# A retention and attention trunk: the ring tiles of split weights start at a place that moves by 16 bytes from product to product

## The chip, the cores and the metric

One core of a Trainium2 chip runs the whole kernel. The time is the device time of one execution in microseconds, from start to end; it is stated as the median of several runs. One more execution was taken with the hardware profiler, and all rows of traces come from that one.

## The reference

Two requests of 512 tokens and width 1024 pass through two layers with the same weights, each `x = x + Mixer(RMSNorm(x))`, and a last RMSNorm. All is fp32.

```python
def diff_attention(h, w_in, lq1, lk1, lq2, lk2, subln_g, w_out, lambda_init):
    proj = h @ w_in                                    # 1024 -> 8192
    q, k, v, gate = jnp.split(proj, [...], axis=-1)
    q = rotary_half(q...) * (DA_HEAD_DIM ** -0.5);  k = rotary_half(k...)
    ...
        p = jax.nn.softmax(s, axis=-1).reshape(B, N_HEADS, 2, Q_BLOCK, S)
        a = (p[:, :, 0] - lam * p[:, :, 1])
        return jnp.einsum('bhqk,bkhe->bqhe', a, v)
    ...
    o = rms_norm(o, subln_g, SUBLN_EPS) * (1.0 - lambda_init)
    return (o * jax.nn.silu(gate)) @ w_out              # 2048 -> 1024

def bidir_retention(h, w_in, decay_fwd, decay_bwd, subln_g, w_out):
    proj = h @ w_in                                    # 1024 -> 6144
    ...
    o_f = retention_direction(q, k, v, log_g_f, True)
    o_b = jnp.flip(retention_direction(flipped q, k, v, log_g_b, False), 1)
    o = rms_norm(o_f + o_b, subln_g, SUBLN_EPS)
    return (o * jax.nn.silu(gate)) @ w_out
```

## The kernel before

**Split operands.** A product of two fp32 matrices is made of three passes in the type float32r. Each operand is split into a high part (a copy on ScalarE, `hi_of`, L400) and a low part (source less high part on VectorE, `lo_of`, L403), and `PASSES` at L32 names the pairs: high by high, high by low, low by high. A matmul on TensorE has a stationary operand, 128 x 128, that a weight load brings in, and a moving one, 128 rows of 256 or 512 columns.

**The two projections.** A unit (`Unit`, from L518 on) is a block of 256 columns of a layer's input weights for both requests. It is computed by seven products P1 to P7 in place of eight, in the manner of Strassen and Winograd: sums of blocks of the activations (B11, B21, T1 to T4, made by `make_b` and kept split in 28 slots for the whole stage) by sums of blocks of weights. `prep` loads the raw weights by DMA, forms the sum in a tile `st` on VectorE (L558) and splits it into tiles of the ring `ws`, of `WS_BUFS` = 7 places with 1024 floats to a partition. `product` issues the matmuls. A "pair" unit has both parts in one ring tile, as the stationary operand, and the activations move, 512 columns (L599, twelve matmuls to a product). A "wide" unit has a ring tile for each part, the activations are stationary, and the ring tiles move, 256 columns (L609, 48 to a product). `evac` takes the sums out of PSUM, through ScalarE copies `c` and VectorE sums `e` (L644), a ring of eight tiles; gates, rotated q and k, and v go out to DRAM.

**Attention and retention.** The first layer goes through head, request and 128 tokens: scores (L1116), softmax, transposes (L1161), weighted sums (L1181). The second goes through blocks of head and request, in two halves of 256 tokens: `state2` (L1339), `score2` (L1315), `av2` (L1359, L1367). Both end in `out_step` (L891), with oT stationary and the split output weights moving, 512 columns: `out_weights` splits these into two ring tiles of `ws` per head and half.

**Where tiles lie.** Pools are laid one behind the other: `sm`, `cp`, `ar`, `wk`. `ar` holds one large tile, the arena, of 18 slots of 1024 floats; `slot` gives a view into it, which starts at

```python
        lo = 32 + at * 1024 + shift
```

with a `shift` in floats: 16 (64 bytes) for the first layer's k and v, 16 and 32 for the second's q and k, 32 for oT (`new_oT`, L826). A slot with a shift reaches into the next one, which `b.also` tells the planner. Other slots, such as those from 20 on, and constants are tiles of `cp`; the rings are tiles of `wk`, made by `view`. Columns that are not a multiple of 16 floats have a pool of their own, `sm`.

**Order.** Nothing is issued in the order of the source. Every operation goes to `Plan.op` with a cost and its reads and writes. `Plan.arrange` makes an order for each engine from these costs, with the places of the rings as limits: a tile can be written anew when the users of the one `bufs` before it are done. Semaphores are then set by the compiler for the order that came out.

Of the kernel before, what the change touches and what calls it, by code (L numbers as in the profile page):

```python
# [9 lines left out]
F32 = mybir.dt.float32  # L10
F32R = mybir.dt.float32r
# [4 lines left out]
P = 128  # L16
S = 512
D = 1024
KT = D // P
NT = S // P  # L20
NH = 8
# [11 lines left out]
WS_BUFS = 7  # L33
# [220 lines left out]
def trunk_kernel(  # L254
# [10 lines left out]
    plan = Plan()  # L265

    sm = ctx.enter_context(tc.tile_pool(name="sm", bufs=1))
    cp = ctx.enter_context(tc.tile_pool(name="cp", bufs=1))
    ar = ctx.enter_context(tc.tile_pool(name="ar", bufs=1))
    wk = ctx.enter_context(tc.tile_pool(name="wk", bufs=1))  # L270
# [2 lines left out]
    dr = ctx.enter_context(tc.tile_pool(name="dr", bufs=1, space=bass.MemoryType.DRAM))  # L273


    SIZE = dict(ws=1024, raw=1024, st=1024, c=512, e=512, m=512, os=1024)
    places = {}
    cnt = [0]

    def view(pool, tag, i, size, shape, dt=F32):  # L280


        if size % 16 and pool in (cp, wk):
            pool = sm
        if (tag, i) not in places:
            places[tag, i] = pool.tile([P, size], F32, tag=f"{tag}{i}", name=f"{tag}_{i}", bufs=1)
        n = math.prod(shape[1:])
        t = places[tag, i][0:shape[0], 0:n]
        if dt != F32:
            t = t.bitcast(dt)  # L290
        if len(shape) == 3:
            t = t.rearrange("p (a b) -> p a b", a=shape[1])
        elif len(shape) == 4:
            t = t.rearrange("p (a b c) -> p a b c", a=shape[1], b=shape[2])
        return t

    def work(tag, shape, bufs, dt=F32, name=None):
        size = SIZE.get(tag, shape[1])
        return Buf(plan, tag, bufs, lambda i: view(wk, tag, i, size, shape, dt))

    arena = ar.tile([P, 18 * 1024 + 80], F32R, tag="arena", name="arena")

    def slot(n, shape, dt=F32R, shift=0):

        size = math.prod(shape[1:])
        at = None if n in (12, 13) or n >= 20 else n if n < 12 else n - 2
        if at is None:
            assert not shift  # L310
            cnt[0] += 1
            label = f"b_{cnt[0]}"
            return Buf(plan, f"b{n}", 1, lambda i: cp.tile(shape, dt, tag=f"b{n}", name=label))
        assert dt == F32R
        lo = 32 + at * 1024 + shift

        def make(i):
            t = arena[:, lo:lo + size]
            return t.rearrange("p (a b) -> p a b", a=shape[1]) if len(shape) == 3 else t
        b = Buf(plan, f"b{n}", 1, make)  # L320
        b.also = Buf(plan, f"edge{at + 1 if shift else at}", 1, None)
        return b

    def const(shape, tag, dt=F32, size=None):
        return Buf(plan, tag, 1, lambda i: view(cp, tag, i, size or math.prod(shape[1:]), shape, dt))

    def ws_t(shape):
        return work("ws", shape, WS_BUFS, F32R)

    def raw_t(shape):  # L330
        return work("raw", shape, 4)

    def st_t(shape, name="st"):
        return work("st", shape, 3, name=name)
# [2 lines left out]
        return work("c", [P, S], 4, name=name)  # L337

    def e_t(name="e"):
        return work("e", [P, S], 8, name=name)  # L340

    def m_t(name="m"):
        return work("m", [P, S], 4, name=name)
# [9 lines left out]
    def bank(tag, name=None):  # L353
        return Buf(plan, tag, BUFS[tag], lambda i: view(pj if tag == "pj" else sc, tag, i, S, [P, S]))
# [16 lines left out]
    def dve(n, fn, r, w, wait=0.0):  # L371
        plan.op("DVE", 0.07 + 0.00104 * n, fn, r, w, wait=wait)
# [20 lines left out]
    def dma(out, in_, r, w, kb, eng=None):  # L393

        q = eng or nc.sync
        plan.op("SP" if eng is None else "ACT", 0.62, lambda: q.dma_start(out(), in_()), r, w, lands=2.0 + kb / 200.0,
                kb=kb, load=any(isinstance(k[0] if isinstance(k, tuple) else k, Buf) for k in w))

    def hi_of(n, dst, src, r, w):
        act(n, lambda: nc.scalar.copy(dst(), src()), r, w)  # L400

    def lo_of(n, dst, src, hi, r, w):
        dve(n, lambda: nc.vector.tensor_tensor(dst(), src(), hi().bitcast(F32), op=ALU.subtract), r, w)  # L403
# [39 lines left out]


    Bop = {}
    powers = const([P, NH, NT], "powers", size=64)

    def make_b(layer, source):

# [39 lines left out]
        for name, h, k0 in (("B11", h11, 0), ("B21", h21, 4)):  # L489
            for k in range(4):  # L490
# [4 lines left out]
                if not (layer == 0):  # L495
                    split(name, k, *h[k])
                yield
        t = [whole(e_t("h")), whole(e_t("h")), half(two[2], 0), half(two[2], 1)]
        for k in range(4):
            ps, scale = source(1, k)  # L500
# [17 lines left out]
    class Unit:  # L518
# [32 lines left out]
        def prep(self, op):  # L551
            x = self.take
            n = 256 if self.wide else P

            def combine(a, b, fn):
                t = st_t([P, 4, n])
                out = ((lambda: self.like(t.t)), t)
                dve(4 * n, lambda: nc.vector.tensor_tensor(out[0](), a[0](), b[0](), op=fn), [a[1], b[1]], [t])  # L558
                return out
            if op == "P1":  # L560
                src = x(0, 0)
            elif op == "P2":
                src = x(0, 1)
            elif op == "P4":
                src = x(1, 1)
            elif op == "P5":
                src = self.s[1] = combine(x(1, 0), x(1, 1), ALU.add)
            elif op == "P6":
                src = self.s[2] = combine(self.s[1], x(0, 0), ALU.subtract)
            elif op == "P3":  # L570
                src = combine(x(0, 1), self.s[2], ALU.subtract)
            else:
                src = combine(x(0, 0), x(1, 0), ALU.subtract)
            if self.wide:
                a, b = ws_t([P, 4, n]), ws_t([P, 4, n])
                hi, lo = ((lambda: a.t), a), ((lambda: b.t), b)
            else:
                s = ws_t([P, 2, 4, n])
                hi, lo = ((lambda: s[:, 0]), (s, 0)), ((lambda: s[:, 1]), (s, 1))
            hi_of(4 * n, lambda: self.like(hi[0]()), src[0], [src[1]], [hi[1]])  # L580
            lo_of(4 * n, lambda: self.like(lo[0]()), src[0], lambda: self.like(hi[0]()), [src[1], hi[1]], [lo[1]])
            self.ops[op] = (hi, lo)
            if op == "P2" and self.early is not None:
                self.early, self.x = None, {}
# [42 lines left out]
        def evac(self, op):  # L627
# [12 lines left out]
            def sums(banks, cs):  # L640
                out = []
                for ps, c in zip(banks, cs):
                    e = e_t()
                    dve(S, lambda e=e, ps=ps, c=c: nc.vector.tensor_tensor(e.t, ps.t, c.t, op=ALU.add), [ps, c], [e])  # L644
                    out.append(e)
                return out
# [177 lines left out]
        return rr  # L824

    def new_oT(g):  # L826
        return [slot(16 + 2 * g + a, [P, 2, S], F32R, 32) for a in range(2)]

    def load_qk(src, i, shift):
        t = slot(i, [P, 2, S], F32R, shift)  # L830
        dma(lambda: t.t.bitcast(F32), lambda: src[0][src[1]], [src[0]], [t], 512)
        return t
# [29 lines left out]
    def out_weights(w, h, i):  # L862
        r = raw_t([P, 2, S])
        src = w[h * 256:(h + 1) * 256, i * S:(i + 1) * S].rearrange("(e p) c -> p e c", p=P)
        dma(lambda: r.t, lambda: src, [], [r], 512)
        hi, lo = ws_t([P, 2, S]), ws_t([P, 2, S])
        hi_of(1024, lambda: hi.t, lambda: r.t, [r], [hi])
        lo_of(1024, lambda: lo.t, lambda: r.t, lambda: hi.t, [r, hi], [lo])
        wsn[h, i] = (hi, lo)
# [58 lines left out]
    qk_d = {}  # L928
# [75 lines left out]
    TURN2 = itertools.cycle(["tp", "o"])  # L1004

    idle = e_t("idle")
    dve(256, lambda: nc.vector.memset(idle.t, 0.0), [], [idle])
    for _ in range(8):
# [84 lines left out]
    qk, vt, sg, oT = {}, {}, {}, {}  # L1093
    st = [{} for _ in tiles]

    def fetch1(h, g, v=True):
        for j in range(2):
            for which in range(2):
                qk[h, g, j, which] = load_qk((qk_d[0, which, h, g], j), 6 * which + 2 * g + j, 16 * which)
        if v:  # L1100
            fetch1_v(h, g)

    def fetch1_v(h, g):
        vt[h, g] = load_v(v_d[0, h, g], 10 + 4 * g, 16)
        sg[h, g] = load_sg(g_d[0, h, g])
# [108 lines left out]
    def at(f, i, n):  # L1214
        if 0 <= i < n:
            f(i)

    fetch1(0, 0)
    fetch1(0, 1, False)
    turns2 = itertools.chain(["sc", "o", "sc", "o"], itertools.cycle(["tp", "o"]))  # L1220
    made = make_b(1, x_source(1, xN, lambda g: next(turns2) if g else "pj"))
# [48 lines left out]
    qk, vt, sg, oT = {}, {}, {}, {}  # L1270
# [78 lines left out]
    def av2(b, c):  # L1349
# [29 lines left out]
        if c == 0:  # L1379
            settle(h - 1, g)  # L1380
            oT[h, g] = new_oT(g)
# [71 lines left out]
    for i in range(N2 + 1):  # L1453
        if i < N2:
            b, c = chunks[i]
# [78 lines left out]
```

## Time and profile before

| | |
|---|---|
| median of 2 runs | 1809.53 us (1809.19 to 1809.87) |
| span of the profiled execution | 1807.0 us |
| TensorE matmuls | 1794.9 us busy, 99%, 10299 instructions |
| weight loads | 1558.1 us busy, 86%, 10299 instructions |
| VectorE | 1477.1 us busy, 82% |
| ScalarE | 895.1 us busy, 50% |
| granted TensorE clock | 0.999 |

The span is the time between the first and the last instruction of the profiled execution; 1809.53 less 1807.0, 2.5 us, lies around it. Matmuls overlap in the pipeline and their ends are modelled, so the busy time of TensorE says that it is never without work, and the distance from one start to the next says what a matmul costs.

### The profile page before, as it was taken

Reading aid. Unit: us, or ns where it says so; the run is one execution under the profiler, and the core shown is the slowest. Engines: PE = TensorE matmul, PEld = TensorE weight load, DVE = VectorE, ACT = ScalarE, POOL = GpSimd, SP = SyncE. Lnnn points to the kernel's source line nnn. Section 1 sums busy time; section 2 is a strip of 40 time slices with the busy share of each in tenths; the row PEclk is TensorE's granted clock in tenths of the full one; section 3 lists DMA queues with packets and bytes.
Section 4 is the critical chain, followed back from the end, with each engine's and each line's share of the span. In section 5 each row is a group of like instructions: output and inputs, shape, how many; then the busy total and the mean of one; then the engine's idle time right before and its main releaser. Section 6 shows DMA issues by size and latency. Waiting matters only on the chain.

```text
span 1807.0 us, 27780 instructions
## 1 busy us (share of the span) xinstructions
PE 1794.9 (99%) x10299; PEld 1558.1 (86%) x10299; DVE 1477.1 (82%) x2319; ACT 895.1 (50%) x1856; POOL 169.5 (9%) x323
## 2 busy tenths in 40 slices
PE   9999999999999999999999999999999999999998
PEld 6789889898988888888888888898989898888887
DVE  7958787778699888888888897787887967888887
ACT  7753444433434565554555866444434355444346
POOL 1000000000000022222322300000000000111113
PEclk9999999999999999999999999999999999999999
DMA  6444455555545685444554524464657559765662
GB/s 217 134 126 137 161 140 178 184 168 155 174 126 175 201 334 198 178 156 159 190 204 140 190 73 146 140 210 146 205 156 228 151 170 396 272 238 182 225 218 94
DMA packets 162767, 328.81 MB, mean 182 GB/s; under 512 B 12724, under 2 KB 76872, under 8 KB 162632
## 3 DMA queue, kind: packets, MB, share of 16 engines
q1 hardware_dynamic: 162304, 326.71, 54.1%
q8 instruction: 81, 1.33, 0.3%
q14 instruction: 54, 0.44, 0.1%
q10 hardware_dynamic: 328, 0.34, 0.1%
HBM read 209.55 MB, written 117.44 MB: 181 GB/s over the span
## 4 chain that ended last, share of the span: by engine, by line
PE 93%; DVE 2%; DMA 2%; ACT 2%; issue 1%; POOL 0%; SPq 0%; POOLq 0%; DVEq 0%; ACTq 0%
PE pj L599 20%; PE pj L891 19%; PE sc L599 10%; PE pj L609 10%; PE o L599 8%; PE o L1181 5%; PE sc L1116 5%; PE sc L609 5%; PE o L609 2%; PE o L1359 2%; PE tp L1161 2%; PE sc L1315 1%; PE o L1367 1%; PE tp L1339 1%; DMA raw<-in_ret_w_out_dram 1%
## 5 line engine op out<-in xcount | busy, mean ns | idle before, releaser
L891 PE MATMUL pj<-ws,arena 128*128 128x512 f32 x1542 | 391.2, 397 | 0.0
L891 PEld LDWEIGHTS pj<-ws,arena 128*128 128x128 f32 x1542 | 277.7, 188 | 52.7
L599 PE MATMUL pj<-b,ws 128*128 128x512 f32 x1080 | 265.0, 392 | 0.0
L599 PEld LDWEIGHTS pj<-b,ws 128*128 128x128 f32 x1080 | 201.4, 188 | 43.0
L403 DVE TENSOR_TENSOR ws<-st,ws 128x512 fp32r<-128x512 f32 (+1 forms) x192 | 147.9, 774 | 74.8 <-ACT ws L400 56.7
L896 DVE SCALAR_TENSOR_TENSOR b<-pj,crr,b 128x512 f32<-128x512 f32 (+1 forms) x257 | 189.9, 744 | 21.4 <-PE pj L891 21.0
L403 DVE TENSOR_TENSOR ws<-raw,ws 128x512 fp32r<-128x512 f32 (+1 forms) x164 | 141.5, 868 | 71.3 <-ACT ws L400 61.0
L400 ACT CAST ws<-st 128x512 fp32r<-128x512 f32 (+1 forms) x192 | 132.4, 693 | 121.4 <-PE pj L599 36.4
L599 PE MATMUL sc<-arena,ws 128*128 128x512 f32 x768 | 186.8, 392 | 0.0
L599 PE MATMUL o<-arena,ws 128*128 128x512 f32 x744 | 180.0, 393 | 1.1 <-ACT m L385 0.6
L599 PEld LDWEIGHTS sc<-arena,ws 128*128 128x128 f32 x768 | 144.0, 188 | 31.3
L400 ACT CAST ws<-raw 128x512 fp32r<-128x512 f32 (+1 forms) x164 | 125.7, 772 | 87.0 <-PE o L599 45.0
L599 PEld LDWEIGHTS o<-arena,ws 128*128 128x128 f32 x744 | 138.4, 188 | 31.7 <-DVE arena L463 1.4
L599 PE MATMUL pj<-arena,ws 128*128 128x512 f32 x648 | 160.3, 392 | 0.4 <-DVE arena L463 0.4
L599 PEld LDWEIGHTS pj<-arena,ws 128*128 128x128 f32 x648 | 120.8, 188 | 26.7 <-DVE arena L463 0.7
L1134 ACT ACTIVATE b<-sc,nm 128x512 f32<-128x512 f32 x128 | 88.0, 689 | 66.9 <-DVE nm L1124 66.5
L636 ACT COPY c<-pj 128x512 f32<-128x512 f32 x104 | 60.9, 586 | 119.7 <-PE pj L599 66.4
L609 PE MATMUL pj<-ws,b 128*128 128x256 f32 x960 | 116.8, 276 | 0.0
L609 PEld LDWEIGHTS pj<-ws,b 128*128 128x128 f32 x960 | 113.2, 188 | 0.7
L1116 PE MATMUL sc<-arena 128*128 128x512 f32 x384 | 101.2, 395 | 0.3 <-ACT b L1134 0.3
L1181 PEld LDWEIGHTS o<-arena 128*128 128x128 f32 x768 | 93.1, 188 | 2.7
L1181 PE MATMUL o<-arena 128*128 128x256 f32 x768 | 93.7, 278 | 0.0
(207 smaller groups left out, 2855.9 us busy)
## 6 DMA issues: line engine op xcount, KB each, us to landing
qk<-os SPq DMA_DIRECT2D x192, 256.0 KB, 3.6
arena<-qk SPq DMA_DIRECT2D x96, 512.0 KB, 5.8
raw<-in_da_w_in_dram SPq DMA_DIRECT2D x64, 512.0 KB, 5.1
v<-os SPq DMA_DIRECT2D x64, 512.0 KB, 4.3
arena<-v SPq DMA_DIRECT2D x64, 512.0 KB, 4.1
raw<-in_ret_w_in_dram SPq DMA_DIRECT2D x48, 512.0 KB, 4.8
os<-g SPq DMA_DIRECT2D x32, 512.0 KB, 7.4
g<-e SPq DMA_DIRECT2D x48, 256.0 KB, 4.6
```

What stands on the lines that cost most here:

```text
L400: act(n, lambda: nc.scalar.copy(dst(), src()), r, w)
L403: dve(n, lambda: nc.vector.tensor_tensor(dst(), src(), hi().bitcast(F32), op=ALU.subtract), r, w)
L599: nc.tensor.matmul(ps.t, a[u][0]()[:, k, :], bt[k][:, v, :], start=(opens and k == 0 and i == 0), stop=(k == 3 and i == 2), skip_group_che ...
L609: nc.tensor.matmul(ps[:, (t % 2) * 256:(t % 2) * 256 + 256], bt[k][:, v, t * P:(t + 1) * P], a[u][0]()[:, k, :], start=(opens and t % 2 == ...
L636: act(S, lambda c=c, ps=ps: nc.scalar.copy(c.t, ps.t), [ps], [c])
L891: nc.tensor.matmul(ps[:, here], o[a][:, e, t * P:(t + 1) * P], u[b][:, e, here], start=(m == 0), stop=(m == 5))
L896: axpy(n, lambda half=half, here=here, ps=ps: nc.vector.scalar_tensor_tensor(half, ps[:, here], rr[:, t % 2:t % 2 + 1], half, op0=ALU.mult ...
L1116: nc.tensor.matmul(s.t, q[:, a, t * P:(t + 1) * P], k[:, b, :], start=(n == 0), stop=(n == 2))
L1134: act(840, lambda j=j, s=s, m=m: nc.scalar.activation(p[:, j, :], s.t, AF.Exp, bias=m.t, accum_out=sm[:, 2 * j + n:2 * j + n + 1]), [s, m] ...
L1161: nc.tensor.transpose(tp[:, j * P:(j + 1) * P], p[:, 0, j * P:(j + 1) * P], ident.t)
L1181: nc.tensor.matmul(o[:, e * 256:(e + 1) * 256], v[b][:, j, e * P:(e + 1) * P], aT[a][:, j, :], start=(n == 0), stop=(n % 12 == 11), skip_g ...
L1359: nc.tensor.matmul(o[:, e * 256:(e + 1) * 256], v_[v][:, 2 * c + j, e * P:(e + 1) * P], a_[:, u, j * 256:(j + 1) * 256], start=(e == 0 and ...
```

## The change

It alters where tiles lie and the length of one ring, and no operation.

- Each product of the projections, and each pair of output weights, takes a number in turn, counted for itself among the pair products, the wide products and the output weights. Its ring tiles are used from the byte 16 x (number mod 16) on. The ring's tiles are 1088 floats long and lie in `ar` behind the arena.
- The arena loses its 32 floats at the front. The first layer's k has no shift any more, oT has one of 64 floats in place of 32.
- Tiles of at most 32 floats become slices of one tile `small`, 192 floats long.
- The ring `e` has seven tiles in place of eight.

```diff
-    SIZE = dict(ws=1024, raw=1024, st=1024, c=512, e=512, m=512, os=1024)
+    SIZE = dict(raw=1024, st=1024, c=512, e=512, m=512, os=1024)
...
-        if size % 16 and pool in (cp, wk):
-            pool = sm
+        n = math.prod(shape[1:])
         if (tag, i) not in places:
-            places[tag, i] = pool.tile([P, size], F32, tag=f"{tag}{i}", name=f"{tag}_{i}", bufs=1)
-        n = math.prod(shape[1:])
+            if size <= 32 and pool in (cp, wk):
+                places[tag, i] = small[:, used[0]:used[0] + size]
+                used[0] += size
+            else:
+                places[tag, i] = pool.tile([P, size], F32, tag=f"{tag}{i}", name=f"{tag}_{i}", bufs=1)
...
-    arena = ar.tile([P, 18 * 1024 + 80], F32R, tag="arena", name="arena")
+    small, used = sm.tile([P, 192], F32, tag="small", name="small"), [0]
+    arena = ar.tile([P, 18 * 1024 + 64], F32R, tag="arena", name="arena")
+    rings = [ar.tile([P, 1024 + 64], F32R, tag=f"ws{i}", name=f"ws_{i}") for i in range(WS_BUFS)]
...
-        lo = 32 + at * 1024 + shift
+        lo = at * 1024 + shift
...
-    def ws_t(shape):
-        return work("ws", shape, WS_BUFS, F32R)
+    def ws_t(shape, turn):
+        lo = 4 * (turn % 16)
+        def make(i):
+            t = rings[i][:, lo:lo + 1024]
+            ...
+        return Buf(plan, "ws", WS_BUFS, make)
+
+    count = dict(pair=0, wide=0, out=0)
...
     def e_t(name="e"):
-        return work("e", [P, S], 8, name=name)
+        return work("e", [P, S], 7, name=name)
...
+            count[self.kind] += 1
             if self.wide:
-                a, b = ws_t([P, 4, n]), ws_t([P, 4, n])
+                a, b = ws_t([P, 4, n], count["wide"]), ws_t([P, 4, n], count["wide"])
...
-                s = ws_t([P, 2, 4, n])
+                s = ws_t([P, 2, 4, n], count["pair"])
...
-        return [slot(16 + 2 * g + a, [P, 2, S], F32R, 32) for a in range(2)]
+        return [slot(16 + 2 * g + a, [P, 2, S], F32R, 64) for a in range(2)]
...
-        hi, lo = ws_t([P, 2, S]), ws_t([P, 2, S])
+        count["out"] += 1
+        hi, lo = ws_t([P, 2, S], count["out"]), ws_t([P, 2, S], count["out"])
...
-                qk[h, g, j, which] = load_qk((qk_d[0, which, h, g], j), 6 * which + 2 * g + j, 16 * which)
+                qk[h, g, j, which] = load_qk((qk_d[0, which, h, g], j), 6 * which + 2 * g + j, 0)
```

More of the change, by code (lines that the diff above doesn't have):

```diff
@@ L325, in const @@
         return Buf(plan, tag, 1, lambda i: view(cp, tag, i, size or math.prod(shape[1:]), shape, dt))
-    def ws_t(shape):
-        return work("ws", shape, WS_BUFS, F32R)
+    def ws_t(shape, turn):
+        lo = 4 * (turn % 16)
+        def make(i):
+            t = rings[i][:, lo:lo + 1024]
+            if len(shape) == 3:
+                return t.rearrange("p (a b) -> p a b", a=shape[1])
+            return t.rearrange("p (a b c) -> p a b c", a=shape[1], b=shape[2])
+        return Buf(plan, "ws", WS_BUFS, make)
+    count = dict(pair=0, wide=0, out=0)
     def raw_t(shape):
@@ L445, in trunk_kernel @@
     Bop = {}
-    powers = const([P, NH, NT], "powers", size=64)
+    powers = const([P, NH, NT], "powers")
     def make_b(layer, source):
```

## The prediction

> **What bounds the kernel now.** The page's shares come first, then the grouped instructions with shapes kept apart, then the chain that ended last, in order of time, in windows of single groups.
>
> ```profile
> span 1807.0 us, 27780 instructions
> ...
> PE 1794.9 (99%) x10299; PEld 1558.1 (86%) x10299; DVE 1477.1 (82%) x2319; ACT 895.1 (50%) x1856; POOL 169.5 (9%) x323
> ...
> PEclk9999999999999999999999999999999999999999
> ...
> PE 93%; DVE 2%; DMA 2%; ACT 2%; issue 1%; POOL 0%; SPq 0%; POOLq 0%; DVEq 0%; ACTq 0%
> ```
>
> TensorE is busy 99% of the span at full granted clock, and 93% of the last-ending chain is TensorE itself. So the time is the sum of the steps from one matmul's start to the next; a wait elsewhere counts only once it reaches TensorE. What does a step cost? The chain's pieces tell it, since a piece of n matmuls is n steps long:
>
> ```profile
> 303.34 2.72 PE sc L609 x24
> ...
> 530.49 2.75 PE pj L599 x12
> ...
> 816.85 2.73 PE o L1181 x24
> 819.58 1.38 PE sc L1116 x6
> ```
>
> A step of 256 columns is 2.72/24 = 113.3 ns, one of 512 columns 2.75/12 = 229.2 ns (1.38/6 = 230 for the scores). Each step also hides one weight load, that of the next matmul: PEld's count equals PE's, and loads are busy for 86% of the span. The change is about where these two reads, the moving rows of matmul i and the weights of matmul i+1, lie in memory. Do steps depend on that at all? The same groups of instructions also occur with longer steps:
>
> ```profile
> 804.60 2.83 PE o L1181 x24
> 807.43 1.40 PE sc L1116 x6
> ```
>
> Here the same 24 attention matmuls take 117.9 ns each and the same six scores 233.3. The groups say how usual that is (mean of one; only differences matter, as the ends are modelled):
>
> ```profile
> L891 PE MATMUL pj<-ws,arena 128*128 128x512 f32 x1530 | 389.8, 398 | 0.0
> L599 PE MATMUL pj<-b,ws 128*128 128x512 f32 x1080 | 265.0, 392 | 0.0
> ...
> L609 PE MATMUL pj<-ws,b 128*128 128x256 f32 x960 | 116.8, 276 | 0.0
> L1116 PE MATMUL sc<-arena 128*128 128x512 f32 x384 | 101.2, 395 | 0.3 <-ACT b L1134 0.3
> L1181 PE MATMUL o<-arena 128*128 128x256 f32 x768 | 93.7, 278 | 0.0
> ...
> L1359 PE MATMUL o<-arena 128*128 128x256 f32 x384 | 48.9, 276 | 0.0
> ...
> L1315 PE MATMUL sc<-arena 128*128 128x256 f32 x192 | 28.0, 282 | 0.1
> ```
>
> L609 and L1359 run at 276, the short step; L1315, the second layer's scores with the same shape, at 282, the long one; L1181 is between. Two speeds, then: a short step and one about 4 ns longer, and the long one is sustained once it has set in. Nothing but TensorE's own reads differs between these groups of one shape, so the place of operands is a candidate, though the trace doesn't prove it.
>
> **The places.** From the sizes of the pools in the two programs, the bytes at which operands start modulo 256 are, before: the projections' split activations at 32, the ring tiles `ws` at 224, oT at 160, and the operands of the attention and retention products at 32, 96 or 160. So the two reads of every product start 64 bytes apart, one way or the other. After: activations, oT, q, k of the first layer at 128; the ring tiles at 0, 16, ... 240 in turn. The distance runs evenly through all 16 multiples; first-layer scores get distance 0; L1181, L1315, L1339, L1359 and L1367 keep 64.
>
> Of the 512-column steps with ring tiles (L599 and L891, 3360 + 1530 = 4890), 906 get a distance of 0 or 16 bytes, 612 stay at 64, 3372 get another; with the 384 scores, 1290 stand at 0 or 16. Of the 256-column ones (L609's 2688 and 12 of L891), 492, 336 and 1872.
>
> **The change part by part.**
>
> *Distances other than 0, 16 and 64.* The trace has no sustained group at such a distance. Nearest are the two speeds. From below the price is 0, the short step stays; a gain of more needs something that the steps now all pay (below, a rival). From above it is the long step for all of them: (2.83 - 2.72)/24 = 4.6 ns for 256 columns against L609's piece, 4.2 against L1181's own, say 4.4; (1.40 - 1.38)/6 = 3.3 ns for 512. I take the upper end, since a group whose start sets it off stays long to its end (24 of 24 steps in the piece at 804.60) and only two of 16 distances are known to start short: 3372 x 3.3 + 1872 x 4.4 = 11.1 + 8.2 = 19 us.
>
> *Distances of 0 and 16.* Here both reads begin in the same place. Single cases are in the trace, where one group of projections follows another of the other kind: the last matmul's moving rows and the next group's weights then both lie at 224 or both at 32.
>
> ```profile
> 189.90 0.91 PE pj L609 x8
> 190.81 2.75 PE pj L599 x12
> 193.55 5.47 PE pj L609 x48
> ```
>
> The pieces are 113.8, 229.2 and 114.0 ns a step, with such a step at the end of the first two: a single one costs nothing that can be read, 0 to 10 ns. That is the lower end. The upper end is that the two reads take turns all along: the weights' 128 columns then delay the moving rows by as many, half of a 256-column step, 113.3/2 = 57 ns. The ends are far apart: a single step speaks for 0, a sustained one is not seen. I take 15 ns, their middle by ratio between the long step's 4 and 57: (1290 + 492) x 15 = 27 us; by the ends 0 and 102 us.
>
> The Trainium skill, TensorE: Matmul & The Clock Gate, on step 1 of "Step-by-step: what each phase is for", gives TensorE two independent read ports, so that loading the next weights takes no read bandwidth from the running matmul. The boundary pieces agree with that; the two speeds of one instruction at one shape are something it doesn't foresee. By it both terms above would be 0; it is taken up below as a rival.
>
> *The ring of sums `e`, eight to seven.* TensorE's list of instructions keeps its 4250 rows and nearly their order; the planner moves a few transposes and scores of the first heads. DVE's and ACT's are reordered locally. What waits on that ring is DVE's sum, and behind it in DVE's queue the splits that TensorE needs. It is hidden by the projections' distance between split and use: TensorE's own idle time at L599's largest group is 0.0. It has one exposed place, the passage between the layers' stages, where gates leave from `e`:
>
> ```profile
> 1510.31 7.85 DMA g<-e
> ...
> 1518.16 0.02 DVEq L1374
> ...
> 1518.53 0.42 DVE b L403
> ...
> 1518.99 0.44 PE tp L815 x2
> ```
>
> ```profile
> 1500.00:1807.00 307.00, 299.77 (x1816) 264.72 (x1816) 263.23 (x435) 144.96 (x382) 48.20 (x79) 0.99 0.61 228
> ```
>
> TensorE idles 307.00 - 299.77 = 7 us in this stretch (its columns are the window, then busy time of PE, PEld, DVE, ACT, POOL). A reordering can win at most these 7 us or, with as long a wait once more, lose 8. I take +1.
>
> *The rest.* Ring tiles 256 bytes larger, the small columns gathered into one tile, oT and arena moved: no instruction and no DMA is added, and waits are as many as before within ten of some 800 on DVE. Writes into ring tiles now start at any 16 bytes: should DVE and ACT take longer for them, DVE's 18% of idle time covers it. Taken as 0.
>
> **Sum.** 19 + 27 + 1 = 47 us on the profiled execution's 1807.0. The median of the runs, 1809.53, lies 2.5 above that span, which is what lies around it, so **1857 us**, 2.6% more.
>
> **Rivals.**
>
> *No dependence on place.* The two speeds come from how a group begins, not from distances. For it: the boundary pieces, and four kinds of products at two different signs of 64 have the same short step. Against: L1315 against L1359, same shape, 6 ns apart. Time: 1809.5 + 1 = 1811. The skill's two ports are this case.
>
> *The reads take turns at 0 and 16.* The upper end: 102 + 19 + 1 = 122, 1932. For it: nothing but that one product in sixteen, and all first-layer scores, now start there. Against: the boundary pieces. It decides from 57 ns a step.
>
> *Faster, by the start of the moving rows.* Every moving row starts 32 bytes into a piece of 64 now (32, 96, 224). Transposes, of 128 columns that pass twice, take 109 ns a step, so 256 passed columns without that start:
>
> ```profile
> 820.96 0.44 PE tp L1161 x4
> ```
>
> 0.44/4 = 110 against 113.3 for 256 and 229.2 for 512: 3.3 and 9.2 ns that might be the price of that start. After the change L599, the scores and all attention products start on a multiple of 64, and a quarter of L609 and L891: (3360 + 384 + 383) x 9.2 + (768 + 960 + 672) x 3.3 = 38 + 8 = 46 us less: 1764. Against: the transposes' own operands start at 32 too, so the start alone can't be it. This is the one on the other side.
>
> *The shorter ring tells.* One more wait as long as the 7.85 us at the passage: 1817.
>
> **How the numbers follow.** Forecast 0.43, turns 0.11, no dependence 0.25, ring 0.08, faster 0.13. A measurement of this kernel can tell about 2% from no change, 36 us: 1773 to 1846. Faster is the one case, 0.13. Slower is turns and 0.39 of the forecast's 0.43, which falls under 36 us when its second term is nearer 0: 0.50. Within: 0.25 + 0.08 + 0.04 = 0.37. The range reaches down past no dependence with some gain at the passage, to 1800, and up to the turns' end and a lost wait, 1935; it leaves out the faster case. The likeliest's own range is 1830 to 1890.
>
> **What would show it.** The forecast: at L599 and L891 the mean of one rises by some 3 to 15 ns, differently from product to product with a period of 16, PE stays at 99%, and the scores (now L1133) rise from 395 to about 410. No dependence: 392 and 276 stay, and so does the scores' 395. Turns: a group of 12 at distance 0 lasts 3.4 us rather than 2.75. Faster: L599 under 385. Ring: steps as now, more idle time before PE at the passage. I am wrong above all if distance 0 costs no more in a sustained group than at a boundary: then the scores say so at once, since all 384 stand there.

## The result and the profile after

The changed kernel takes **1836.13 us** (1835.68 to 1836.58) against 1809.53 for the kernel before: a ratio of 1.0149, interval 1.0119 to 1.0178. So the change costs 27 us, 1.5%, where 47 us were forecast. Now to where they are. First the page of the changed kernel:

```profile
span 1834.8 us, 27786 instructions
...
PE 1821.7 (99%) x10299; PEld 1573.8 (86%) x10299; DVE 1479.5 (81%) x2319; ACT 896.1 (49%) x1856; POOL 171.5 (9%) x323
...
PEclk9999999999999999999999999999999999999999
...
PE 95%; DMA 2%; DVE 2%; issue 1%; ACT 1%; POOL 0%; SPq 0%; POOLq 0%; ACTq 0%; DVEq 0%
```

TensorE's busy time rose from 1794.9 to 1821.7, by 26.8 us; the span less that busy time rose from 12.1 to 13.1. The same 10299 matmuls, at a granted clock of 0.998 where it was 0.999, with next to no more waiting, take longer each. The groups, shapes kept apart, tell which:

```profile
L908 PE MATMUL pj<-ws,arena 128*128 128x512 f32 x1530 | 392.7, 400 | 0.0
L615 PE MATMUL pj<-b,ws 128*128 128x512 f32 x1080 | 268.0, 395 | 0.2 <-DVE e L660 0.2
...
L625 PE MATMUL pj<-ws,b 128*128 128x256 f32 x960 | 120.8, 280 | 0.0
L1133 PE MATMUL sc<-arena 128*128 128x512 f32 x384 | 100.5, 395 | 0.3 <-ACT b L1151 0.3
...
L1376 PE MATMUL o<-arena 128*128 128x256 f32 x384 | 50.1, 279 | 0.0
```

Against before, L615 (L599 before) rose from 392 to 395 ns, L625 (L609) from 276 to 280, L908 (L891) from 398 to 400, L1376 (L1359) from 276 to 279. L1133, the first layer's scores, all of which now have a distance of 0, stayed at 395.

Nearly all ring products changed their distance, and the chain in order of time shows what each distance does. Two windows of it:

```profile
280.81 2.74 PE o L615 x12
283.54 2.72 PE sc L615 x12
286.26 2.73 PE pj L615 x12
288.99 2.79 PE sc L615 x12
...
314.40 5.72 PE pj L625 x48
320.12 5.45 PE sc L625 x48
325.57 5.72 PE pj L625 x48
```

With the address of every operand set beside its matmul, the four pieces of L615 have distances of 240, 0, 16 and 32 bytes, and their steps are 2.74/12 = 228.3, 226.7, 227.5 and 232.5 ns. The three of L625 stand at 80, 64 and 48: 119.2, 113.5, 119.2 ns. "Distance" is from here on the weights of matmul i+1 less the moving rows of matmul i, modulo 256, with its sign: 64 bytes forward is 64, 64 back is 192. Inside a product it is the same for every step; where one product follows another, the step between them can have a distance of its own. In these terms, before the change the pairs and the output products stood at 192 and the wides at 64.

Averaged over all steps of a line but those over 330 ns, in which TensorE waited or ran at a lower clock, start to start, in ns, each step under the distance of its own product (the two columns "alone" come from the experiment with TensorE alone below, a piece's length by 48):

| distance | 512 columns, L615 | alone | 256 columns, L625 | alone |
|---|---|---|---|---|
| 0 | 227.5 | 227.3 | 119.7 | 120.0 |
| 16 | 228.5 | 226.9 | 117.3 | 118.3 |
| 32 | 232.7 | 233.1 | 118.3 | 118.3 |
| 48 | 233.1 | 233.3 | 119.9 | 117.7 |
| 64 | 233.6 | 233.1 | **113.6** | **113.5** |
| 80 | 232.4 | 231.9 | 119.7 | 118.8 |
| 96, 112 | 234.6, 234.0 | 234.2, 233.3 | 117.8, 118.6 | 118.8, 120.0 |
| 128 | 233.8 | 233.3 | 118.9 | 118.5 |
| 144 | 234.8 | 233.3 | **113.8** | 120.0 |
| 160 | 232.9 | 233.1 | 120.0 | 120.0 |
| 176 | 231.0 | 229.9 | 119.5 | 118.1 |
| 192 | 229.7 | 229.0 | 118.0 | 113.3 |
| 208, 224 | 233.0, 233.3 | 233.1, 233.3 | 118.3, 117.2 | 116.7, 116.7 |
| 240 | 228.9 | 227.1 | 118.2 | 119.8 |

Before, the 512-column steps of L599 had 229.5 in the mean and the 256-column ones of L609 113.7. So the change took the wides from one of the two distances that are good for them in this kernel and spread them over sixteen, and the pairs from a good one to sixteen of which four are as good or better.

### The profile page after: what moved, and what is told of

Its sections match the earlier page's. It is cut to its first block, busy times and chain, and to the rows that moved or that the text cites. A ratio compares the mean times of both kernels' runs of the same rounds, so it can differ in the third digit from the quotient of the medians.

```text
span 1834.8 us, 27786 instructions
## 1 busy us (share of the span) xinstructions
PE 1821.7 (99%) x10299; PEld 1573.8 (86%) x10299; DVE 1479.5 (81%) x2319; ACT 896.1 (49%) x1856; POOL 171.5 (9%) x323
## 4 chain that ended last, share of the span: by engine, by line
PE 95%; DMA 2%; DVE 2%; issue 1%; ACT 1%; POOL 0%; SPq 0%; POOLq 0%; ACTq 0%; DVEq 0%
PE pj L615 20%; PE pj L908 19%; PE sc L615 11%; PE pj L625 10%; PE o L615 9%; PE sc L625 5%; PE o L1198 5%; PE sc L1133 4%; PE o L625 2%; PE o L1376 2%; PE tp L1178 1%; PE sc L1332 1%; PE o L1384 1%; PE tp L1356 1%; DMA raw<-in_da_w_out_dram 1%
## 5 line engine op out<-in xcount | busy, mean ns | idle before, releaser
L908 PE MATMUL pj<-ws,arena 128*128 128x512 f32 x1542 | 394.2, 399 | 0.0
L908 PEld LDWEIGHTS pj<-ws,arena 128*128 128x128 f32 x1542 | 277.8, 188 | 53.9
L615 PE MATMUL pj<-b,ws 128*128 128x512 f32 x1080 | 268.0, 395 | 0.2 <-DVE e L660 0.2
L615 PEld LDWEIGHTS pj<-b,ws 128*128 128x128 f32 x1080 | 201.6, 188 | 46.2 <-DVE e L660 0.7
L913 DVE SCALAR_TENSOR_TENSOR b<-pj,small,b 128x512 f32<-128x512 f32 (+1 forms) x257 | 190.4, 746 | 25.3 <-PE pj L908 23.9
L615 PE MATMUL sc<-arena,ws 128*128 128x512 f32 x768 | 188.8, 394 | 0.0
L615 PE MATMUL o<-arena,ws 128*128 128x512 f32 x744 | 183.3, 398 | 0.9 <-ACT m L400 0.6
L615 PEld LDWEIGHTS sc<-arena,ws 128*128 128x128 f32 x768 | 144.1, 188 | 33.2
L615 PEld LDWEIGHTS o<-arena,ws 128*128 128x128 f32 x744 | 139.6, 190 | 33.5 <-DVE arena L478 1.0
L615 PE MATMUL pj<-arena,ws 128*128 128x512 f32 x648 | 162.0, 394 | 0.4 <-DVE arena L478 0.4
L615 PEld LDWEIGHTS pj<-arena,ws 128*128 128x128 f32 x648 | 121.0, 188 | 28.3 <-DVE arena L478 0.7
L1151 ACT ACTIVATE b<-sc,small 128x512 f32<-128x512 f32 x128 | 87.9, 689 | 69.9 <-DVE small L1141 69.0
L625 PE MATMUL pj<-ws,b 128*128 128x256 f32 x960 | 120.8, 280 | 0.0
L625 PEld LDWEIGHTS pj<-ws,b 128*128 128x128 f32 x960 | 117.0, 188 | 0.7
L1133 PE MATMUL sc<-arena 128*128 128x512 f32 x384 | 100.5, 395 | 0.3 <-ACT b L1151 0.3
L1198 PEld LDWEIGHTS o<-arena 128*128 128x128 f32 x768 | 93.3, 188 | 3.4 <-ACT arena L415 0.7
L1198 PE MATMUL o<-arena 128*128 128x256 f32 x768 | 94.1, 279 | 0.5 <-ACT arena L415 0.5
```

Of the source, the lines that this page charges most:

```text
L615: nc.tensor.matmul(ps.t, a[u][0]()[:, k, :], bt[k][:, v, :], start=(opens and k == 0 and i == 0), stop=(k == 3 and i == 2), skip_group_che ...
L625: nc.tensor.matmul(ps[:, (t % 2) * 256:(t % 2) * 256 + 256], bt[k][:, v, t * P:(t + 1) * P], a[u][0]()[:, k, :], start=(opens and t % 2 == ...
L908: nc.tensor.matmul(ps[:, here], o[a][:, e, t * P:(t + 1) * P], u[b][:, e, here], start=(m == 0), stop=(m == 5))
L913: axpy(n, lambda half=half, here=here, ps=ps: nc.vector.scalar_tensor_tensor(half, ps[:, here], rr[:, t % 2:t % 2 + 1], half, op0=ALU.mult ...
L1133: nc.tensor.matmul(s.t, q[:, a, t * P:(t + 1) * P], k[:, b, :], start=(n == 0), stop=(n == 2))
L1151: act(840, lambda j=j, s=s, m=m: nc.scalar.activation(p[:, j, :], s.t, AF.Exp, bias=m.t, accum_out=sm[:, 2 * j + n:2 * j + n + 1]), [s, m] ...
```

## The experiments

**The ring of sums alone.** The kernel before, with seven tiles in `e`:

```diff
-        return work("e", [P, S], 8, name=name)
+        return work("e", [P, S], 7, name=name)
```

> The kernel before with the ring of sums at seven tiles in place of eight and nothing else. Theory 'place': 1809 to 1811. Theory 'layout and ring': a part of the 26.6 us, up to 1836.

1809.12 us, ratio 0.9995 (0.9986 to 1.0004). The shorter ring by itself costs nothing in the kernel before. Whether the 27 us belong to the places of the ring tiles is asked by the runs that follow.

**Fixed turns instead of running ones.** Three runs put constants where the product's number stood. In the changed kernel the ring tiles begin 128 bytes past a multiple of 256, and I had taken them to begin at one, in the prediction too (there it changes nothing, as the running turns pass through all sixteen places); so the distances that the three expectations name are not those that ran. A turn t gives 16t to the pairs and -16t to the wides and output products (modulo 256).

```diff
-                a, b = ws_t([P, 4, n], count["wide"]), ws_t([P, 4, n], count["wide"])
+                a, b = ws_t([P, 4, n], 4), ws_t([P, 4, n], 4)
...
-                s = ws_t([P, 2, 4, n], count["pair"])
+                s = ws_t([P, 2, 4, n], 4)
...
-        hi, lo = ws_t([P, 2, S], count["out"]), ws_t([P, 2, S], count["out"])
+        hi, lo = ws_t([P, 2, S], 12), ws_t([P, 2, S], 12)
```

> The changed kernel with the ring tiles held at one place per kind, at the distances (weights less moving rows, modulo 256) of the kernel before: pairs 192, wides 64, output weights 192; ring of seven sums, the gathered columns and scores at distance 0 stay. Theory 'place' (each step's length follows from the distance of its two reads): 1808 to 1812 us, groups L615 at 392 and L625 at 276. Theory 'layout and ring' (seven sums, larger tiles, writes at other places): stays at 1830 to 1838.

What ran: pairs 64, wides 192, output products 64; every ring product's distance of before with its sign turned. 1839.83 us, ratio 1.0163 (1.0144 to 1.0182), slower than the running turns.

```diff
+                a, b = ws_t([P, 4, n], 4), ws_t([P, 4, n], 4)
...
+                s = ws_t([P, 2, 4, n], 8)
...
+        hi, lo = ws_t([P, 2, S], 8), ws_t([P, 2, S], 8)
```

> As e1, but pairs and output weights at distance 0 and wides at 64, the places with the shortest steps in the changed kernel's trace (226.7 and 113.3 ns). Theory 'place': 3360 x 2.4 = 8 us from pairs and 1530 x 2 to 4 = 3 to 6 from output products below the kernel before, 1795 to 1800. Theory of the prediction's second term ('both reads in one place cost 15 ns or more a step once sustained'): 1809.5 + 4890 x 15 = 1883 or more.

What ran: pairs 128, wides 192, output products 128. 1840.0 us, 1.0165 (1.0149 to 1.0181).

```diff
+                a, b = ws_t([P, 4, n], 0), ws_t([P, 4, n], 0)
...
+                s = ws_t([P, 2, 4, n], 14)
...
+        hi, lo = ws_t([P, 2, S], 1), ws_t([P, 2, S], 1)
```

> As e1, but each kind held at a distance with long steps: pairs 96 (234.5 ns), wides 128 (119.7), output weights 112. Theory 'place': 3360 x 5 + 2688 x 6.3 + 1530 x 3 = 17 + 17 + 5 us above the kernel before, 1845 to 1852. Theory 'the turning itself' (steps are long because the place changes from product to product and settle when it is held): 1808 to 1815.

What ran: pairs 224, wides 0, output products 240. 1844.64 us, 1.0191 (1.0174 to 1.0207).

As tests of the expectations these three failed; as measurements they serve. The first says that, for these pairs and wides, a distance of 64 is not the same as one of 192. Its chain where the kernel before has 5.44 for each wide piece and 2.75 for each pair (window from 300 us on):

```profile
314.99 5.65 PE pj L625 x48
320.65 5.65 PE sc L625 x48
326.30 5.65 PE pj L625 x48
331.95 2.80 PE pj L615 x12
```

117.7 ns a wide step and 233.3 a pair step, where before had 113.3 and 229.2. The third puts all wides at 0: L625's group of 960 is at 283 ns, 122.9 us busy, the longest of all runs, while at that distance the pairs are shortest. The steps also add up: against before, the third's 2688 wide steps are 6.3 ns longer (120.0), its 3360 pair steps 4.2 (233.7) and its 1530 output steps 1.3, which is 16.9 + 14.1 + 2.0 = 33 us, and the second layer's products give 2 more; measured are 35.5 over the 1809.17 beside it.

**The distances of before, in the changed kernel.**

```diff
+                a, b = ws_t([P, 4, n], 12), ws_t([P, 4, n], 12)
...
+                s = ws_t([P, 2, 4, n], 12)
...
+        hi, lo = ws_t([P, 2, S], 4), ws_t([P, 2, S], 4)
```

> The changed kernel with the ring tiles held at the distances of the kernel before, mended: ring tiles begin at 128 modulo 256, which e1 to e3 had not reckoned with, so that e1 had in truth pairs at 64, wides at 192, output weights at 64, e2 128, 192, 128, and e3 224, 0, 240. Here pairs are at 192, wides at 64, output weights at 192. Theory 'place by distance': 1808 to 1813 us, L615 at 392 and L625 at 276. Theory 'layout' (what else changed: seven sums, gathered columns, absolute places, writes): 1836 to 1840 like e1.

Pairs 192, wides 64, output products 192: 1812.45 us, ratio 1.0017 (1.0008 to 1.0026). Of the 27 us, 24 are gone, with the larger tiles, the shifted arena, the short ring and the one tile of small columns all still there.

```profile
L615 PE MATMUL pj<-b,ws 128*128 128x512 f32 x1080 | 265.0, 392 | 0.2 <-DVE e L660 0.2
...
L625 PE MATMUL pj<-ws,b 128*128 128x256 f32 x960 | 116.8, 276 | 0.0
...
L1376 PE MATMUL o<-arena 128*128 128x256 f32 x384 | 50.2, 279 | 0.0
```

L615 and L625 have their busy times of before back to 0.1 us. L1376 has not (48.9 us and 276 ns before), though neither its own places nor its distance of 192 depend on the turns. So the 3 us that are left, 2.1 of them in L1376 and its neighbour L1384, hang on something besides the distance.

**The absolute place.** The kernel before, one small column more, which moves every tile behind it by 32 bytes and leaves each distance as it was (with the ring of seven):

```diff
+    pad = sm.tile([P, 1], F32, tag="pad", name="pad", bufs=1)
+    dve(1, lambda: nc.vector.memset(pad, 0.0), [], [(pad, 0)])
...
-        return work("e", [P, S], 8, name=name)
+        return work("e", [P, S], 7, name=name)
```

> The kernel before with seven sums, and one more small column, so that all operands lie 32 bytes further on: moving rows start on multiples of 64 bytes, distances are unchanged. Theory 'place by distance': 1807 to 1812. Theory of the prediction's faster rival (the start within 64 bytes is what costs): 1764. Theory 'absolute place': slower, towards 1836, as the changed kernel's operands also start on multiples of 64.

1809.64 us, 1.0002 (0.9993 to 1.0011). Moving rows now start on multiples of 64 and nothing changes.

**TensorE alone.** A program that leaves out the whole trunk: 48 matmuls at each of 16 distances, for four places of the moving rows (bytes 128, 160, 0, 96 modulo 256; the last letter p, q, r, s), with 512 columns (l) and 256 (s); the middle letter a to p is the distance in units of 16 bytes. No DMA and no other engine runs beside it, and the granted clock was 1.0. In outline:

```diff
+        for p in range(4):
+            for d in range(16):
+                for n in range(48):
+                    nc.tensor.matmul(bank, w[...from 16 * d bytes past the moving rows...], m[..., 512 columns])
+        ...the same with 256 columns
```

> TensorE alone, on one loaded tile, outputs left at zero: 48 matmuls in the passes of a pair (512 columns) and of a wide (256 columns) for each of 16 distances and four places of the moving rows (128, 160, 0, 96 modulo 256); no transfer and no other engine runs beside them. Theory 'place by distance': the same steps as in the changed kernel, 512 columns 226.7 ns at 0, 16 and 240, 229.2 at 192, 231 to 235 elsewhere; 256 columns 113.3 at 64 and 144, 117 to 120 elsewhere; the same at all four places. Theory 'the other engines' reads and writes or the transfers take part': one short step for all distances. Theory 'absolute place': the list of distances differs from place to place.

The chain in order of time:

```profile
18.31 10.89 PE lbp L297 x48
...
51.58 11.19 PE lep L297 x48
...
140.97 10.99 PE lmp L297 x48
...
174.36 10.91 PE lpp L297 x48
...
551.92 10.89 PE lbs L297 x48
...
741.63 5.45 PE sep L305 x48
...
769.92 5.76 PE sjp L305 x48
...
787.11 5.44 PE smp L305 x48
```

At 16 and 240 bytes (b, p) a 512-column step is 226.9 to 227.3 ns, at 192 (m) 229.0, at 64 (e) 233.1; with 256 columns 64 and 192 take 113.5 and 113.3, 144 (j) 120.0. The piece at 16 bytes is 10.89 us long at the first place (p) and at the last (s), and the others repeat in the same way (only the first piece of all, 12.89 us, is longer and stands in no column above): the step goes by the distance, not by the place, and it needs no other engine. Each piece is entered from the one 16 bytes below it, at all four places alike. One thing differs from the kernels: 256 columns at 192 are short here and 118.0 in the changed kernel, and 144 is the reverse.

**Pairs at 0.** By the table, distance 0 should shorten the pairs.

```diff
+                a, b = ws_t([P, 4, n], 12), ws_t([P, 4, n], 12)
...
+                s = ws_t([P, 2, 4, n], 0)
...
+        hi, lo = ws_t([P, 2, S], 4), ws_t([P, 2, S], 4)
```

> As e5, with the pairs at distance 0. Theory 'place by distance', from the changed kernel's own groups at 0 (226.8 ns a step against 229.2): 3360 x 2.4 = 8 us below e5, 1800 to 1805. Theory of the prediction's second term (both reads in one place, 15 ns a step): e5 + 50 = 1860.

1816.83 us, 1.0043 (1.003 to 1.0056): 4.4 us more than with the pairs at 192.

```profile
L615 PE MATMUL pj<-b,ws 128*128 128x512 f32 x1080 | 263.0, 390 | 0.2 <-DVE e L660 0.2
...
L625 PE MATMUL pj<-ws,b 128*128 128x256 f32 x960 | 120.9, 281 | 0.0
```

```profile
321.16 5.65 PE pj L625 x48
326.81 2.72 PE pj L615 x12
329.53 5.65 PE pj L625 x48
```

The pairs came out short, 2.72/12 = 226.7, about 2 ns below 229.5 in the mean and 6.5 us over 3360 of them. But the wides, whose distance of 64 was not touched, went from 113.7 to 117.7 in the mean, and that is 2688 x 4.0 = 11 us. With the output products at 0 as well:

```diff
-        hi, lo = ws_t([P, 2, S], 4), ws_t([P, 2, S], 4)
+        hi, lo = ws_t([P, 2, S], 0), ws_t([P, 2, S], 0)
```

> As e6, with the output weights at distance 0 too. Theory 'place by distance': groups of six do not settle (steps 226 to 237 at the group's start), so within 4 us of e6 either way. Theory of the second term: e6 + 23.

1817.13 us, 1.0043 (1.0031 to 1.0056), and the same again on a smaller scale:

```profile
L908 PE MATMUL pj<-ws,arena 128*128 128x512 f32 x1530 | 388.5, 397 | 0.0
...
L1133 PE MATMUL sc<-arena 128*128 128x512 f32 x384 | 99.8, 393 | 0.2 <-ACT b L1151 0.2
L1198 PE MATMUL o<-arena 128*128 128x256 f32 x768 | 95.8, 281 | 0.5 <-ACT arena L415 0.5
```

L908 gains 1.6 us over the run before (390.1), the scores 0.8; the attention products at 64 that follow them, L1198, lose 2.5 (93.3). It looks as if a product's step depended on its distance and on what ran ahead of it; the next run asks TensorE alone.

**Pairs, then wides, with TensorE alone.** Again without the trunk, at a granted clock of 1.0: 24 steps of 512 columns, then 48 of 256, twice each, for five distances of the pairs (second letter: a 0, b 16, p 240, m 192, l 176) and all 16 of the wides (third letter).

```diff
+        for dp in (0, 1, 15, 12, 11):
+            for dw in range(16):
+                for turn in range(2):
+                    ...24 matmuls of 512 columns at distance 16 * dp
+                    ...48 matmuls of 256 columns at distance 16 * dw
```

> TensorE alone as in b1, outputs left at zero: 24 matmuls of a pair (512 columns) and 48 of a wide (256 columns) in turn, twice, for pairs at distance 0, 16, 240, 192 and 176 with wides at each of 16 distances. It asks why the wides of e6 stand at 117.7 ns a step at the very distance, 64, at which those of e5 stand at 113.3. Theory 'the step's length is handed on where the kinds change': wides at 64 take 117.7 after pairs at 0, 113.3 after pairs at 192; some other pairing may join 226.7 to 113.3. Theory 'something else in e6 lengthens them' (other engines, transfers): wides at 64 take 113.3 after every kind of pair.

```profile
96.84 5.45 PE lae L296 x24
102.29 5.65 PE sae L305 x48
...
219.17 5.47 PE laj L296 x24
224.64 5.48 PE saj L305 x48
...
1169.76 5.49 PE lme L296 x24
1175.26 5.47 PE sme L305 x48
```

Behind pairs at 192 (m) wides at 64 (e) are short, 5.47/48 = 114.0; behind pairs at 0 (a) the same wides are long, 117.7, through all 48 steps. Behind pairs at 0 it is the wides at 144 (j) that are short, 114.2. So a run of steps settles in its first ten or so into a speed that is decided at its entry, and keeps that to its end.

The other groups of this run say how far that goes. The wides at 144 are short behind all five distances of the pairs, 114.1 to 114.5 in all ten groups, though the pieces at 144 had 120.0 in the first run of TensorE alone, entered from 128. The wides at 64 are short both times behind pairs at 192 and long both times behind 0, but behind 16, 240 and 176 short once and long once. Pairs at 16 take 227 ns a step in some groups and 233 in others. So the distance of the run before doesn't settle the speed by itself either. Short for both kinds in both turns are pairs at 192 with wides at 64, and wides at 144 with pairs at 0, 16, 240 and 192.

**The pairing in the kernel.** Pairs 0, wides 144, output products 192:

```diff
+                a, b = ws_t([P, 4, n], 7), ws_t([P, 4, n], 7)
...
+                s = ws_t([P, 2, 4, n], 0)
...
+        hi, lo = ws_t([P, 2, S], 4), ws_t([P, 2, S], 4)
```

> The kernel after with fixed places: products of the pairs at distance 0, wide products at 144 (instead of 64), output products at 192; no turns; everything else as in the kernel after. Theory A, a step's length goes by the distance and by the speed that the run of products is entered with: the measurement of TensorE alone had 226.7 ns for pairs at 0 and 113.5 ns for wides at 144 right behind them, where wides at 64 took 117.8. Then against the run with pairs 192, wides 64 (1812.45 us): 3360 products of the pairs at about 2.0 ns less are 6.7 us less, wides unchanged, about 1806 us, between 1804 and 1808; the group of the pairs at 227.5 ns a step, the wides at 113.6 to 114. This would be faster than before by about 0.2%. Theory B, the pairing holds only where TensorE works alone, and in the kernel the wides behind pairs at 0 are long whatever their distance: about 117.7 ns a wide step and 1816 to 1818 us, as with pairs 0 and wides 64.

1806.97 us, ratio 0.9991 (0.9982 to 1.0), inside the 1804 to 1808 of theory A and 9 us under theory B's lower end.

```profile
L615 PE MATMUL pj<-b,ws 128*128 128x512 f32 x1080 | 263.1, 390 | 0.2 <-DVE e L660 0.2
...
L625 PE MATMUL pj<-ws,b 128*128 128x256 f32 x960 | 116.9, 275 | 0.0
```

Both groups are short at once. Then with three more edits: oT 128 bytes back; the output products' ring tiles moved by as much, which keeps their distance at 192; and the first layer's scores at 192 again.

```diff
-        return [slot(16 + 2 * g + a, [P, 2, S], F32R, 64) for a in range(2)]
+        return [slot(16 + 2 * g + a, [P, 2, S], F32R, 32) for a in range(2)]
...
-        hi, lo = ws_t([P, 2, S], 4), ws_t([P, 2, S], 4)
+        hi, lo = ws_t([P, 2, S], 12), ws_t([P, 2, S], 12)
...
-                qk[h, g, j, which] = load_qk((qk_d[0, which, h, g], j), 6 * which + 2 * g + j, 0)
+                qk[h, g, j, which] = load_qk((qk_d[0, which, h, g], j), 6 * which + 2 * g + j, 16 * which)
```

> As the run with pairs 0 and wides 144, and three more places as before the change: the two shifts of the stationary and moving tiles outside the ring (the output products again 192 apart, with the arena's tiles of oT shifted by 32 words; the first layer's scores again at 192 instead of 0). Theory A, steps go by distance and by the speed handed on at entry: the output products stay at 192; the scores of the first layer lose the 0.9 ns a step that distance 0 gave them; the second layer's products at 192 go back from 117 to 118 to 113.6 ns if the places entered before them decide that, which is 2.5 to 3 us less: 1802 to 1806 us, against 1804 to 1808 without these places. If the second layer's products are entered from the pairs at 0 in any case, they stay at 117 to 118 ns and the time is that of the run with pairs 0 and wides 144 within 2 us. Theory B, the pairing does not hold in the kernel: 1814 to 1818 us.

1804.57 us, ratio 0.9976 (0.9966 to 0.9985). This is faster than both kernels, by 4.2 and by some 32 us.

```profile
L1198 PE MATMUL o<-arena 128*128 128x256 f32 x768 | 94.5, 279 | 0.0
...
L1376 PE MATMUL o<-arena 128*128 128x256 f32 x384 | 48.8, 276 | 0.0
...
L1384 PE MATMUL o<-arena,b 128*128 128x256 f32 x192 | 27.0, 276 | 0.0
```

L1376 and L1384 are back at 276 ns, with their own distance of 192 unchanged. The traces show where it comes from. These products run in groups of 18, mostly behind six output products (L908), and the step into a group has a distance of its own: the group's first weights less the last moving rows of L908, which are a ring tile. In the run before it is 192 and here 64, behind output products at 192 both times. One such group in the run before:

```profile
1669.57 1.41 PE o L1376 x12
1670.98 0.71 PE o L1384 x6
```

and one here:

```profile
1648.70 1.36 PE o L1376 x12
1650.06 0.68 PE o L1384 x6
```

That is 117.8 and 113.3 ns a step. Of the 29 groups behind output products, 28 are long in the run before and 28 short here; the kernel before, with 64 too, has 28 short, and the run with the distances of before, with 192, has 28 long, which is where 2 of its 3 us went. In the changed kernel this step in takes eight distances in turn, and the four groups entered at 80 have 113.3 ns, the 25 others 117.7 to 118.1. It doesn't decide alone either: in the first run with fixed turns it was 64 as well, but behind output products at 64, and all 29 groups were long. L1198 rose from 93.3 to 94.5 us: its groups behind output products went from 114.5 to 116.8 ns, where the same ring tiles took the step in from 0 to 128. What the edit to the first layer's scores does by itself was not separated.

## Why the prediction was right or wrong

The time, 1836.13, lies in the range and 21 us under the forecast; at 1.5% it falls in the class within 2%, which had 0.37, and not in the likeliest, slower by more, which had 0.50. The mechanism was right: the step depends on the distance of the two reads. The excess over before was made of these terms, each as the sum of (step after less the line's mean before), steps over 330 ns left out:

| term | predicted | measured |
|---|---|---|
| distances other than 0, 16 and 64 | 11.1 + 8.2 = 19 us | 11.3 + 8.5 = 19.8 us |
| distances of 0 and 16, one way or the other | 27 us | -0.8 + 2.2 = 1.5 us |
| distance still 64, one way or the other | 0 | 1.0 + 3.3 = 4.3 us |
| the ring `e` | +1 us | 0, the run with it alone is at 0.9995 |

The first three make 25.6 of the 27.8 us by which the matmuls' steps grew in all. Of the rest, 2 us are in steps over 330 ns. Most of that has nothing to do with places: between 27.6 and 31.0 us of the profiled execution the granted clock was 0.51, where the trace of before has it in full, and eight steps of L615 took 425 to 465 ns, 1.6 us more than usual.

*Distances other than 0, 16 and 64.* Right in size: the upper end was taken, the long step for nearly all, and in the mean it is what they pay. The two speeds seen in the trace of before gave that price, though the trace of before had no sustained group at any of these distances. That the mean price came out so near, 3.4 and 4.6 ns where 3.3 and 4.4 were taken, is in part luck: there is not one long step but a price for each distance, from 1.5 ns (176) to 5.3 (144) at 512 columns in L615, and from nothing (144) to 6.3 (160) at 256 columns.

*Distances of 0 and 16.* This is the step that failed: "I take 15 ns, their middle by ratio between the long step's 4 and 57". The idea behind it was that two reads at the same place collide. There is nothing of that: 512 columns are at their shortest at distance 0 and 16, 226.7 to 228.5 ns, and the largest price at 256 columns is 6 ns at 0, not 57. The boundary pieces that I quoted for the lower end had it right, 0 to 10 ns; a middle by ratio towards an end that no row showed made 27 us out of 1.5. The forecast with the lower end would have been 1830.

*Distance of 64.* Put down as unchanged, "one way or the other". The sign counts: 64 and 192 are two distances, and each suits another shape in the kernel, pairs at 192 and wides at 64. The run with these signs turned took 1839.83. And a step that keeps its distance need not keep its length: the second layer's products kept even their sign and lost 2 us, by the step into their groups. The trace of before had this already: L609 and L1315 both stood at 64, with the same shape, and took 113.7 and 118.4 ns.

*The ring, the rest.* As predicted, nothing, but for the +1. That the other edits cost next to nothing rests on the run with the distances of before, within its 3 us, of which 2 belong to the step into the second layer's groups.

**The rivals.** *No dependence on place* falls by the changed kernel itself and by TensorE alone, where one instruction takes 113.3 to 120.0 ns by the distance. The Trainium skill, TensorE: Matmul & The Clock Gate, "Step-by-step: what each phase is for", has two independent read ports, so that loading weights takes nothing from the running matmul; the boundary pieces seemed to agree, and these steps, which go by the distance between the two reads with all else idle, do not. *The reads take turns* falls by 2.72 us for the twelve matmuls at 283.54 us, where it wanted 3.4. *Faster, by the start of the moving rows* falls by the kernel moved 32 bytes on, 1.0002, and by L615 at 395, where it wanted under 385. (That 128 transposed columns count as 256 was only an inference from 110 ns against 113.3.) *The shorter ring* falls by the run with it alone.

**What was to show it.** L615 rose by 3 ns, the lower edge of "3 to 15", and L908 by 2, under it, with the period of 16 that was named; the scores did not go to 410 but stayed at 395, which had been named as the sign that the second term is wrong.

## What to carry to other kernels

When TensorE is the bound and its steps are back to back, look for two speeds of one instruction in the trace before costing a change of layout: here the two were close to the mean price of the unknown distances, though the single prices differ, and a bound that no row shows should not pull an estimate away from a row that does. Fix the distance between the weights and the moving rows on purpose, at a pair of values that suits both kinds of product in turn (here 192 with 64, or 0 with 144; between the best and the worst choice tried lie 40 us of 1810), and measure the pair in the kernel itself, as the step from one kind to the next counts too; a place that walks through all of them pays for the bad ones. And work out addresses from where a tile is put, not from where its pool seems to begin: three runs here measured other places than they were meant to.

## What the runs showed of the hardware

With TensorE alone and its clock granted in full, the step of a 512-column float32r matmul with its weight load goes from 226.9 to 234.2 ns with the distance of weights and moving rows modulo 256 bytes, and that of a 256-column one from 113.3 to 120.0; the place itself, at the four tried, does not count. I had expected the worst at distance 0, and for 512 columns it is among the best there, with 16 and 240.

The length of a step is not fixed by the distance alone: wides at 64 take 113.3 to 114.0 or 117.7 ns according to whether the pairs before them stood at 192 or at 0, and once settled keep that to the end of their 48 steps. The products of L1376 and L1384, at 192 always, take 113.4 or 117.8 ns according to the step into their group and the distance ahead of it. Behind pairs at 16, 240 and 176, wides at 64 had both speeds, so more is handed on there than the distance of the run before. What state of the machine that is, and why these distances are the good ones, no run here shows.
